# Splitting the last two weight tiles of each part into memory outside the ring, so that part ends split no weights

## The chip, the cores and the metric
One core of one Trainium2 chip runs the whole program. The metric is device time in microseconds; smaller is better. Three timed runs of the kernel before took 1474.11, 1475.65 and 1478.8 us (median 1475.65).

## What is computed
Two layers over a sequence of 256 tokens, width 1024, all in float32. Cut to what matters:

```python
for l in range(2):
    x = x + 0.5 * rms_norm(swiglu(rms_norm(x, ffn1_pre_g), ffn1_w_gu, ffn1_w_down), ffn1_post_g)
    x = x + rms_norm(hybrid_mixer(rms_norm(x, mix_pre_g), ...), mix_post_g)     # GLA, S5, forgetting attention
    x = x + rms_norm(memory_cross_attention(rms_norm(x, xa_pre_g), rms_norm(mem, xa_mem_g), ...), xa_post_g)
    x = x + 0.5 * rms_norm(swiglu(rms_norm(x, ffn2_pre_g), ffn2_w_gu, ffn2_w_down), ffn2_post_g)
```

## The kernel before
Each float32 matrix product is made of three products of two rounded halves: `mm3` multiplies high by high, high by low and low by high. So every weight has to be split into two halves on the chip, and that is a steady work beside the matmuls. `make_plan` lists all weights in the order of use as tiles of 128 x 1024. `fetch` brings a tile by a DMA on SyncE's queue into one of `WF` = 5 raw buffers (`wf`). `split_next` casts it on ScalarE to the high half `wh` (L221) and subtracts that from the raw tile to get the low half `wl` (L222), on VectorE (DVE) unless a caller names GpSimd (POOL). The two halves live in a ring of `WB` = 7 tile pairs. `take` hands out the next pair to the matmuls, `free` gives it back, and `ahead`, called between groups of matmuls, splits until the ring holds one pair less than it can (`lag=1`). Every engine does its instructions in the order in which the program lists them; nothing is rescheduled.

A layer has four parts, and each ends at a norm: the first FFN, the mixer up to `w_mix`, the cross attention (`xa`), the second FFN. The end of a part is `boundary`. The last `TAIL` = 5 weight tiles of the part are held together: `go_tail(0)` makes with them the last rows for tokens 0 to 127, `go_tail(1)` those for tokens 128 to 255. While the second runs, ACT, DVE and POOL make the norm of the first half of the tokens (`early`): squares of the finished banks (`junk`, L363), their sum (`rv`, L369), its power -1/2 on GpSimd (`rr`, L370), gain (`nw`, L382), residual sum (`x`, L394), the next norm (L401, L404), scaling (L409) and transposes on TensorE (L415), whose results are split into `xth` and `xtl`. The same chain for the second half (`late`) runs while TensorE makes the next part's first products for the first half (`head`, `go(0)`, L318: four weight tiles). Just before the end of `go(0)` (a hook at 46 of its 48 units of 256 columns) TensorE needs the scaled second half for the transposes `turn(1, 0)`; then `go(1)` follows.

With 5 tiles of the tail in a ring of 7, only two of the four head tiles can be split ahead of the tail. The third is split in `early` by

```python
            self.split_next(nc.gpsimd)
```

once the tail's first tile is given back, and the fourth by the same line ahead of `self.head(width)`. After the mixer there is no head: `fill` makes the first two key projections of the cross attention (`xa_key`, result `kT`) with four tiles `xa_k`, while `late` runs. There the third tile is split on GpSimd, the fourth on DVE, and while `self.pool_every = 4` every fourth tile that no caller names an engine for goes to GpSimd too. `merge_last`, ahead of the `w_mix` products, splits two tiles on GpSimd in each layer, and `first`, at the start of the program, two.

There are seven such boundaries: five with a head (after both FFNs of layer 0, the first of layer 1, and both cross attentions) and two with the fill (after both mixers). The second FFN of layer 1 ends in `store`.

## Time and profile before

| | |
|---|---|
| median of three runs | 1475.65 us |
| the profiled execution | 1474.54 us |
| its span, first to last instruction | 1472.8 us |
| mean granted TensorE clock | 0.989 |
| TensorE busy | 1428.6 us (97%) |
| VectorE busy | 937.3 us (64%) |
| ScalarE busy | 716.3 us (49%) |
| GpSimd busy | 121.2 us (8%) |
| DMA | 257.52 MB, mean 175 GB/s |

The profile is one execution. "Busy" is the sum of the instructions' times on an engine. A share tells little here: TensorE is busy at all but a few places, so what matters are the waits of TensorE and the granted clock behind them. 1474.54 us of the execution less 1472.8 us of span is 1.74 us around the program, in which no instruction of it lies.

### The profile page before, as it was taken

Reading aid. Unit: us, or ns where it says so; the run is one execution under the profiler, and the core shown is the slowest. Engines: PE = TensorE matmul, PEld = TensorE weight load, DVE = VectorE, ACT = ScalarE, POOL = GpSimd, SP = SyncE. Lnnn points to the kernel's source line nnn. Section 1 sums busy time; section 2 is a strip of 40 time slices with the busy share of each in tenths; the row PEclk is TensorE's granted clock in tenths of the full one; section 3 lists DMA queues with packets and bytes.
Section 4 is the critical chain, followed back from the end, with each engine's and each line's share of the span. In section 5 each row is a group of like instructions: output and inputs, shape, how many; then the busy total and the mean of one; then the engine's idle time right before and its main releaser. Section 6 shows DMA issues by size and latency. Waiting matters only on the chain.

```text
span 1472.8 us, 24677 instructions
## 1 busy us (share of the span) xinstructions
PE 1428.6 (97%) x9972; PEld 1318.5 (90%) x9972; DVE 937.3 (64%) x1388; ACT 716.3 (49%) x1129; POOL 121.2 (8%) x80
## 2 busy tenths in 40 slices
PE   8999998999999999999999999989999999999998
PEld 7999978889979989999999999788999798899997
DVE  6787566755486666555578675666556866665553
ACT  5444446355455545444454544454544644454442
POOL 1000020001141020000010000200012400200000
PEclk9999999999999999999999999999999999999999
DMA  7664636255546436555455555362565464275551
GB/s 280 214 199 148 211 108 213 92 156 181 192 173 231 156 113 232 193 178 188 156 181 207 171 200 187 117 191 90 158 229 175 154 216 158 91 248 190 180 192 45
DMA packets 76034, 257.52 MB, mean 175 GB/s; under 512 B 8688, under 2 KB 11792, under 8 KB 75920
## 3 DMA queue, kind: packets, MB, share of 16 engines
q1 hardware_dynamic: 75920, 255.95, 52.2%
q8 instruction: 78, 1.28, 0.3%
q14 instruction: 36, 0.29, 0.1%
HBM read 253.82 MB, written 2.10 MB: 174 GB/s over the span
## 4 chain that ended last, share of the span: by engine, by line
PE 85%; DVE 6%; ACT 4%; issue 2%; DMA 1%; POOL 1%; SPq 0%; DVEq 0%; POOLq 0%; ACTq 0%
PE mm L232 55%; PE pa L232 22%; PE mm L318 3%; DVE wl L222 2%; DVE x L394 1%; ACT wh L221 1%; PE mm L415 1%; DMA fq<-in_onehot 1%; ACT junk L363 1%; PE mm L1033 1%; DVE acc L1193 1%; PE mm L707 1%; DVE xtl L222 0%; PE mm L890 0%; PE pa L925 0%
## 5 line engine op out<-in xcount | busy, mean ns | idle before, releaser
L222 DVE TENSOR_TENSOR wl<-wf,wh 128x1024 fp32r<-128x1024 f32 x432 | 525.1, 1227 | 271.7 <-ACT wh L221 270.6
L232 PE MATMUL mm<-xth,wh 128*128 128x256 f32 (+1 forms) x2000 | 569.9, 285 | 0.0
L232 PE MATMUL mm<-xth,wl 128*128 128x256 f32 (+1 forms) x2000 | 567.2, 284 | 0.0
L232 PE MATMUL mm<-xtl,wh 128*128 128x256 f32 (+1 forms) x2000 | 566.2, 283 | 0.0
L221 ACT CAST wh<-wf 128x1024 fp32r<-128x1024 f32 (+1 forms) x458 | 463.0, 1030 | 161.1 <-PE mm L232 67.7
L232 PEld LDWEIGHTS mm<-xth,wh 128*128 128x128 f32 (+1 forms) x2000 | 378.7, 189 | 4.0 <-issue 2.1
L232 PEld LDWEIGHTS mm<-xtl,wh 128*128 128x128 f32 (+1 forms) x2000 | 376.9, 188 | 1.8
L232 PEld LDWEIGHTS mm<-xth,wl 128*128 128x128 f32 (+1 forms) x2000 | 377.5, 189 | 0.0
L232 PE MATMUL pa<-wh,hl 128*128 128x512 f32 x352 | 137.7, 391 | 0.0
L232 PE MATMUL pa<-wl,hh 128*128 128x512 f32 x352 | 137.6, 391 | 0.0
L232 PE MATMUL pa<-wh,hh 128*128 128x512 f32 x352 | 137.5, 391 | 0.0
L370 POOL TENSOR_TENSOR rr<-rv,mhalf 128x1 f32<-128x1 f32 x36 | 27.9, 775 | 885.5 <-DVE rv L369 876.7
L538 ACT ACTIVATE sil<-mm 128x256 f32<-128x256 f32 (+1 forms) x96 | 35.0, 365 | 127.3 <-PE mm L232 119.8
L540 DVE TENSOR_TENSOR h<-sil,mm 128x256 f32<-128x256 f32 (+1 forms) x96 | 38.0, 396 | 64.3 <-ACT sil L538 64.3
L232 PEld LDWEIGHTS pa<-wh,hl 128*128 128x128 f32 x352 | 66.1, 188 | 14.0
L232 PEld LDWEIGHTS pa<-wl,hh 128*128 128x128 f32 x352 | 66.1, 188 | 12.8
L232 PEld LDWEIGHTS pa<-wh,hh 128*128 128x128 f32 x352 | 66.2, 188 | 12.6
L221 ACT CAST hh<-h 128x256 fp32r<-128x256 f32 x80 | 32.5, 406 | 91.7 <-DVE h L540 91.7
L222 POOL TENSOR_TENSOR wl<-wf,wh 128x1024 fp32r<-128x1024 f32 x26 | 68.6, 2638 | 78.8 <-ACT wh L221 78.8
L222 DVE TENSOR_TENSOR hl<-h,hh 128x256 fp32r<-128x256 f32 x80 | 34.0, 425 | 37.8 <-ACT hh L221 37.8
L232 PE MATMUL pa<-wl,xth 128*128 128x512 f32 x128 | 50.9, 397 | 2.8 <-DVE wl L222 2.7
L232 PE MATMUL mm<-mt,wh 128*128 128x256 f32 x256 | 48.0, 290 | 5.1 <-DVE kT L222 5.1
(274 smaller groups left out, 1701.4 us busy)
## 6 DMA issues: line engine op xcount, KB each, us to landing
wf<-in_ffn_gu SPq DMA_DIRECT2D x176, 512.0 KB, 4.3
wf<-in_ffn_dn SPq DMA_DIRECT2D x88, 512.0 KB, 4.3
wf<-in_w_cols SPq DMA_DIRECT2D x72, 512.0 KB, 4.0
wf<-in_w_mix SPq DMA_DIRECT2D x16, 512.0 KB, 4.4
wf<-in_xa_k SPq DMA_DIRECT2D x16, 512.0 KB, 4.4
wf<-in_xa_q SPq DMA_DIRECT2D x16, 512.0 KB, 4.7
wf<-in_xa_v SPq DMA_DIRECT2D x16, 512.0 KB, 4.4
wf<-in_xa_o SPq DMA_DIRECT2D x16, 512.0 KB, 4.8
```

The source lines that it names most:

```text
L221: self.nc.scalar.copy(h, src)
L222: (eng or self.nc.vector).tensor_tensor(full(lo), src, h.bitcast(F32), op=ALU.subtract)
L232: self.nc.tensor.matmul(out, lhsT=lhs[i], rhs=rhs[j], start=start and n == 0, stop=stop and n == 2)
L318: self.nc.tensor.matmul(out, lhsT=xt[b][:, kk, tk], rhs=w[2 * g + i][a][:, k * width:(k + 1) * width], start=first, stop=last)
L363: self.nc.scalar.activation(jk, src, AF.Square, scale=math.sqrt(f / D), accum_out=s)
L370: self.nc.gpsimd.tensor_tensor(r, v, self.mhalf[:, 0:1], op=ALU.pow)
L394: self.nc.vector.scalar_tensor_tensor(xx, o, r, xx, op0=ALU.mult, op1=ALU.add)
L415: self.nc.tensor.transpose(ps[:, i * 128:(i + 1) * 128], hn[:, k * 128:(k + 1) * 128], self.ident)
L538: nc.scalar.activation(sil, gate, AF.Silu)
L540: nc.vector.tensor_tensor(h, sil, up, op=ALU.mult)
L707: T.matmul(ps[0:32, j * 128:(j + 1) * 128], lhsT=cz[:, i, 4 * q + j], rhs=wa[:, i, 4 * q + j].rearrange("p k h -> p (k h)"), start=i == 0, ...
L1033: T.matmul(o[:, 0:256], lhsT=fv[:, 0, c], rhs=p[:, 0:256], start=True, stop=False)
```

## The change
`make_plan` notes where each of the parts ends in the list of tiles. `house` gives the last two tiles of a part a home outside the ring: in the FFNs the tiles `e0`, `e1`, `e2` of the FFN's pool (in the first FFN these are also scratch of `s5_setup`, under new tags), after the mixer the places of `acc`, `m1` and `fv`, after the cross attention those of the keys (`foh`, `fol`, `fq`, `fk`). A tile with a home takes no place in the ring: `room` lets it be split whenever it is next, and only tiles in the ring are counted (`n_ring`). The `split_next` calls in `boundary` and `pool_every` are gone; the new `ahead(0)` at its start fills the ring.

```diff
+    def house(self, homes):
+        at = self.parts.pop(0)
+        for n, home in enumerate(homes):
+            self.homes[at - len(homes) + n] = home
+
+    def room(self, lag=0):
+        return self.n_split < len(self.plan) and (self.n_split in self.homes or self.n_ring < WB - lag)
...
-        assert i < self.n_free + WB
+        assert self.room()
...
-        h = self.wp.tile([128, HALF], F32R, tag="wh", name="wh")
-        lo = self.wp.tile([128, HALF], F32R, tag="wl", name="wl")
+        if i in self.homes:
+            h, lo = self.homes[i]()
+        else:
+            self.n_ring += 1
+            h = self.wp.tile([128, HALF], F32R, tag="wh", name="wh")
+            lo = self.wp.tile([128, HALF], F32R, tag="wl", name="wl")
...
     def ahead(self, lag=1):
-        while self.n_split < min(len(self.plan), self.n_free + WB - lag):
+        while self.room(lag):
             self.split_next()
...
-        while self.n_split < min(len(self.plan), self.n_free + WB):
-            self.split_next()
+        self.ahead(0)
         go_tail(0)
...
             st["p1"][0](0)
-            self.split_next(nc.gpsimd)
             self.scale(h0, r0)
...
         if fill is not None:
-            self.split_next()
             late()
...
-        self.split_next(nc.gpsimd)
         ps, go = self.head(width)
...
+        self.house((two_halves, lambda: [pool.tile([128, HALF], F32R, tag=n, name="we") for n in ("e1", "e2")]))
...
+        self.house([lambda ns=ns: [com.tile([128, HALF], F32R, tag=n, name="we") for n in ns]
+                    for ns in (("foh", "fol"), ("fq", "fk"))])
...
-                    self.pool_every = 4
+                    self.house((mix_home, lambda: [p.tile([128, HALF], F32R, tag=n, name="we")
+                                                   for p, n in ((self.per, "m1"), (com, "fv"))]))
```

GpSimd's order, from the first boundary to the first fill of layer 0. Before (`rr` is the power -1/2, `wl` a split, `acc` a sum of the mixer):

```order
L370 TENSOR_TENSOR rr<-rv,mhalf 128x1 x2
L222 TENSOR_TENSOR wl<-wf,wh 128x1024
L370 TENSOR_TENSOR rr<-rv,mhalf 128x1
L222 TENSOR_TENSOR wl<-wf,wh 128x1024
L370 TENSOR_TENSOR rr<-rv,mhalf 128x1
L860 TENSOR_TENSOR orr<-ov,mhalf 128x8
```

and with the change (lines have moved by 18 to 20):

```order
L388 TENSOR_TENSOR rr<-rv,mhalf 128x1 x4
L880 TENSOR_TENSOR orr<-ov,mhalf 128x8
```

Both splits have left the boundary. In the whole program 20 of GpSimd's 26 splits are gone; the two of `first` and the four of `merge_last` stay.

VectorE's order at the end of the first mixer, from the last split of the mixer's output (`xtl`) to the residual sum of the first half. Before (`mt` is the transposed memory, `nw<-pa,gain` the first step of the boundary's chain):

```order
L1190 SCALAR_TENSOR_TENSOR xtl<-acc,xth 128x512
L222 TENSOR_TENSOR wl<-wf,wh 128x1024 x2
L222 TENSOR_TENSOR mt<-mm,mt 128x4x128 x2
L222 TENSOR_TENSOR wl<-wf,wh 128x1024
L222 TENSOR_TENSOR mt<-mm,mt 128x4x128 x2
L222 TENSOR_TENSOR wl<-wf,wh 128x1024
L382 TENSOR_TENSOR nw<-pa,gain 128x512
L369 TENSOR_SCALAR rv<-ss 128x1
L382 TENSOR_TENSOR nw<-pa,gain 128x512
L394 SCALAR_TENSOR_TENSOR x<-nw,rr,x 128x512 x2
```

and with the change (`we` is a tile in a home):

```order
L1210 SCALAR_TENSOR_TENSOR xtl<-acc,xth 128x512
L240 TENSOR_TENSOR wl<-wf,wh 128x1024 x2
L240 TENSOR_TENSOR we<-wf,we 128x1024 x2
L240 TENSOR_TENSOR wl<-wf,wh 128x1024
L240 TENSOR_TENSOR mt<-mm,mt 128x4x128 x2
L240 TENSOR_TENSOR wl<-wf,wh 128x1024
L240 TENSOR_TENSOR mt<-mm,mt 128x4x128 x2
L240 TENSOR_TENSOR wl<-wf,wh 128x1024 x2
L400 TENSOR_TENSOR nw<-pa,gain 128x512
L387 TENSOR_SCALAR rv<-ss 128x1
L400 TENSOR_TENSOR nw<-pa,gain 128x512
L412 SCALAR_TENSOR_TENSOR x<-nw,rr,x 128x512 x2
```

Eight splits stand here on VectorE instead of four, five of them ahead of the first `mt`.

VectorE's order after the scaling of the second half in the same boundary, up to the second `kT`. Before:

```order
L222 TENSOR_TENSOR wl<-wf,wh 128x1024
L394 SCALAR_TENSOR_TENSOR x<-nw,rr,x 128x512 x2
L401 TENSOR_TENSOR nw<-x,gain 128x512
L369 TENSOR_SCALAR rv<-ss 128x1
L404 TENSOR_TENSOR nw<-x,gain 128x512
L409 TENSOR_SCALAR nw<-nw,rr 128x512 x2
L222 TENSOR_TENSOR wl<-wf,wh 128x1024 x3
L222 TENSOR_TENSOR kT<-mm,kT 128x512
L222 TENSOR_TENSOR wl<-wf,wh 128x1024
L222 TENSOR_TENSOR kT<-mm,kT 128x512
```

and with the change:

```order
L412 SCALAR_TENSOR_TENSOR x<-nw,rr,x 128x512 x2
L419 TENSOR_TENSOR nw<-x,gain 128x512
L387 TENSOR_SCALAR rv<-ss 128x1
L422 TENSOR_TENSOR nw<-x,gain 128x512
L427 TENSOR_SCALAR nw<-nw,rr 128x512 x2
L240 TENSOR_TENSOR wl<-wf,wh 128x1024 x4
L240 TENSOR_TENSOR kT<-mm,kT 128x512
L240 TENSOR_TENSOR wl<-wf,wh 128x1024 x2
L240 TENSOR_TENSOR kT<-mm,kT 128x512
```

The split ahead of the second `x` has gone; ahead of the two `kT` six splits stand on VectorE instead of four (before, two of the six were GpSimd's).

## Rows read from the trace of the kernel before

**Rows 1.** The page: the span, and busy time of the engines with share of the span and instructions.
```profile
span 1472.8 us, 24677 instructions
PE 1428.6 (97%) x9972; PEld 1318.5 (90%) x9972; DVE 937.3 (64%) x1388; ACT 716.3 (49%) x1129; POOL 121.2 (8%) x80
```

**Rows 2.** Waits of TensorE by what ended them: us in total, times, longest us.
```profile
PE mm L415 <- DVE nw L409: 11.8, 5, 2.5
```

**Rows 3.** TensorE in order of time: the first instruction after a wait, at the five heads (L415), in the tail of the first mixer (425.62), and at the third key projection of both fills (451.59 and 1179.69). Columns: start us, us, engine, line, operation, shapes, count; in brackets the idle time before it and what ended it.
```profile
217.57 0.66 PE L415 MATMUL mm<-cst,nw 128*128 128x128 f32 x4 [2.50 <-DVE nw L409]
552.72 1.09 PE L415 MATMUL mm<-cst,nw 128*128 128x128 f32 x4 [2.21 <-DVE nw L409]
745.98 0.63 PE L415 MATMUL mm<-cst,nw 128*128 128x128 f32 x4 [2.33 <-DVE nw L409]
944.84 0.84 PE L415 MATMUL mm<-cst,nw 128*128 128x128 f32 x4 [2.50 <-DVE nw L409]
1282.30 0.63 PE L415 MATMUL mm<-cst,nw 128*128 128x128 f32 x4 [2.21 <-DVE nw L409]
425.62 0.50 PE L232 MATMUL pa<-wl,xth 128*128 128x512 f32 x1 [1.37 <-DVE wl L222]
451.59 0.50 PE L232 MATMUL mm<-mt,wh 128*128 128x256 f32 x2 [1.52 <-DVE kT L222]
1179.69 0.50 PE L232 MATMUL mm<-mt,wh 128*128 128x256 f32 x2 [3.63 <-DVE kT L222]
```

**Rows 4.** VectorE and GpSimd in order of time at the first boundary: the residual sums of the first and the second half of the tokens, and a split on GpSimd. Columns as in rows 3.
```profile
203.71 1.41 DVE L394 SCALAR_TENSOR_TENSOR x<-nw,rr,x 128x512 f32<-128x512 f32 x2
211.38 3.55 DVE L394 SCALAR_TENSOR_TENSOR x<-nw,rr,x 128x512 f32<-128x512 f32 x2
...
211.51 2.86 POOL L222 TENSOR_TENSOR wl<-wf,wh 128x1024 fp32r<-128x1024 f32 x1 [0.54 <-ACT wh L221]
```

**Rows 5.** The residual sums of the whole run, by line: count, then shortest, median and longest of one in ns, first and last start in us.
```profile
L394 DVE SCALAR_TENSOR_TENSOR x<-nw,rr,x x28: 741/746/2893, 203.7 to 1276.7; 128x512 f32<-128x512 f32 x28
```

**Rows 6.** Stretches of TensorE: start and end in us, length, busy us of PE, PEld, DVE, ACT and POOL with their instructions, then the granted clock, DMA share and GB/s. In order: the first boundary (512 wide) from the transposes of the first half to the wait, and from the wait to the end of `go(1)`; the same two at the second boundary (256 wide); behind the wait of the first fill; behind that of the second.
```profile
207.89:215.07 7.18, 7.18 (x35) 5.51 (x34) 6.64 (x9) 3.47 (x8) 5.95 (x3) 1.00 0.21 73
217.57:225.90 8.33, 8.32 (x33) 6.80 (x34) 6.62 (x8) 6.09 (x8) 0.00 (x0) 0.80 0.36 112
542.80:550.51 7.71, 7.69 (x58) 6.88 (x56) 6.74 (x9) 3.76 (x8) 5.79 (x3) 1.00 0.21 72
552.72:561.17 8.45, 8.45 (x58) 8.45 (x59) 6.12 (x7) 5.91 (x7) 0.00 (x0) 0.80 0.23 72
451.59:453.60 2.01, 2.01 (x16) 2.01 (x17) 1.07 (x1) 1.11 (x2) 0.00 (x0) 1.00 0.94 253
1179.69:1184.20 4.51, 4.51 (x25) 4.51 (x26) 4.00 (x5) 0.65 (x1) 0.00 (x0) 0.62 0.88 301
```

**Rows 7.** The chain that ended last: a tail of the first FFN, 57 matmuls of 512 columns. Start us, us, what.
```profile
195.09 12.96 PE pa L232 x57
```

**Rows 8.** The splits by engine and shape: count, busy us, mean ns of one, idle time before them and what ended it.
```profile
L222 DVE TENSOR_TENSOR wl<-wf,wh 128x1024 fp32r<-128x1024 f32 x414 | 513.3, 1250 | 253.6 <-ACT wh L221 252.5
L222 POOL TENSOR_TENSOR wl<-wf,wh 128x1024 fp32r<-128x1024 f32 x26 | 68.6, 2638 | 78.8 <-ACT wh L221 78.8
```

**Rows 9.** ScalarE in order of time at the end of the first mixer: the casts of the fourth to sixth `w_mix` tile (counted from 0), and those of two `xa_k` tiles, ahead of the first square of the boundary. Columns as in rows 3.
```profile
417.58 2.94 ACT L221 CAST wh<-wf 128x1024 fp32r<-128x1024 f32 x3
423.27 2.01 ACT L221 CAST wh<-wf 128x1024 fp32r<-128x1024 f32 x2
426.39 0.60 ACT L363 ACTIVATE junk<-pa 128x512 bf16<-128x512 f32 x1 [1.10 <-PE pa L232]
```

**Rows 10.** VectorE at the same boundary: a split, the first gain, the two residual sums with their scalings, and the splits ahead of `kT`.
```profile
418.65 1.22 DVE L222 TENSOR_TENSOR wl<-wf,wh 128x1024 fp32r<-128x1024 f32 x1 [0.25 <-ACT wh L221]
428.83 0.68 DVE L382 TENSOR_TENSOR nw<-pa,gain 128x512 f32<-128x512 f32 x1
431.53 1.42 DVE L394 SCALAR_TENSOR_TENSOR x<-nw,rr,x 128x512 f32<-128x512 f32 x2
435.14 0.88 DVE L409 TENSOR_SCALAR nw<-nw,rr 128x512 f32<-128x512 f32 x2 [0.44 <-POOL rr L370]
440.82 1.41 DVE L394 SCALAR_TENSOR_TENSOR x<-nw,rr,x 128x512 f32<-128x512 f32 x2
444.42 0.88 DVE L409 TENSOR_SCALAR nw<-nw,rr 128x512 f32<-128x512 f32 x2 [0.44 <-POOL rr L370]
445.22 5.71 DVE L222 TENSOR_TENSOR wl<-wf,wh 128x1024 fp32r<-128x1024 f32 x3
```

**Rows 11.** TensorE there: the transposes of the first half (the hook of the tail), and the start of the first key projection.
```profile
435.95 0.60 PE L415 MATMUL mm<-cst,nw 128*128 128x128 f32 x4
437.44 0.48 PE L232 MATMUL mm<-mt,wh 128*128 128x256 f32 x2
```

**Rows 12.** DMA issues of the page: count, KB each, median us from issue to landing; and SyncE's longest wait for splits of GpSimd (us in total, times, longest us).
```profile
wf<-in_xa_k SPq DMA_DIRECT2D x16, 512.0 KB, 4.4
...
SPq L147 <- POOL wl L222: 133.3, 24, 12.7
```

**Rows 13.** The end of the values' projection in the first cross attention: VectorE's low halves of the second half of `v`, and TensorE's first product that reads them.
```profile
518.45 1.38 DVE L222 TENSOR_TENSOR v<-mm,v 128x512 fp32r<-128x512 f32 x2 [0.31 <-ACT v L221]
...
521.12 1.59 PE L232 MATMUL mm<-pt,v 128*128 128x256 f32 x12
```

More of the change, by code (lines that the diff above doesn't have):

```diff
@@ L80, in make_plan @@
         a = self.a
-        self.plan = []
+        self.plan, self.parts = [], []
         def add(ap, n=2048):
@@ L98, in ffn @@
                 add(dn[l, k], D)
+            self.parts.append(len(self.plan))
         for l in range(depth):
@@ L133, in make_plan @@
                 add(a["w_mix"][l, q])
+            self.parts.append(len(self.plan))
             for n in ("xa_k", "xa_q", "xa_v", "xa_o"):
@@ L136, in make_plan @@
                     add(a[n][l, q])
+            self.parts.append(len(self.plan))
             ffn(l, 2)
-        self.n_dma = self.n_split = self.n_take = self.n_free = 0
-        self.raw, self.ready = {}, {}
+        self.n_dma = self.n_split = self.n_take = self.n_free = self.n_ring = 0
+        self.raw, self.ready, self.homes = {}, {}, {}
         self.pool_every = 0
+    def house(self, homes):
[4 more added lines that the diff above has]
+        return self.n_split < len(self.plan) and (self.n_split in self.homes or self.n_ring < WB - lag)
     def fetch(self, upto):
@@ L177, in free @@
     def free(self, n=1):
-        self.n_free += n
+        for _ in range(n):
+            self.n_ring -= self.n_free not in self.homes
+            self.n_free += 1
     def start(self, gen, first=False):
@@ L528, in ffn, with two_halves @@
         hs = [None] * NFT
+        def two_halves():
+            t = pool.tile([128, 2, HALF], F32R, tag="e0", name="we")
+            return t[:, 0], t[:, 1]
+        self.house((two_halves, lambda: [pool.tile([128, HALF], F32R, tag=n, name="we") for n in ("e1", "e2")]))
         def split_h(j, src):
@@ L671, in times @@
                 3).to_broadcast([128, 8, m, 32])
-        wa = t8(2, 8, 4, 32)
-        w1, w2 = t8(8, 4, 32), t8(8, 4, 32)
+        wa = pool.tile([128, 2, 8, 4, 32], F32, tag="e0", name="wa")
+        w1, w2 = [pool.tile([128, 8, 4, 32], F32, tag=n, name=n) for n in ("e1", "e2")]
         a3, b3 = w1[:, :, 0:3], w2[:, :, 0:3]
@@ L1342, in run, with mix_home @@
                     pairs = [(xt[0][:, k], xt[1][:, k]) for k in range(KT)]
-                    self.pool_every = 4
+                    def mix_home():
+                        t = lp.tile([128, 2, HALF], F32R, tag="acc", name="we")
+                        return t[:, 0], t[:, 1]
+                    self.house((mix_home, lambda: [p.tile([128, HALF], F32R, tag=n, name="we")
+                                                   for p, n in ((self.per, "m1"), (com, "fv"))]))
                     for k in range(0, KT - TAIL, 2):
@@ L1349, in run @@
                     xt, _ = self.boundary(banks, tail, False, fill=lambda q: self.xa_key(q, mt, kt))
-                    self.pool_every = 0
                     self.start(self.gains(a["xa_post_g"][l], a["ffn2_pre_g"][l]))
```

## Prediction, made before the changed kernel was run
> **What bounds the kernel now.** I read the page first. TensorE is busy in 97% of the span and VectorE in 64% [rows 1], so the change can only be worth what TensorE loses at particular places, and VectorE has room for more work if it comes where nobody waits. The waits of TensorE by what ended them come next: the largest group is the transposes of the second half, which wait for VectorE's scaling, 11.8 us in five waits [rows 2]. In order of time these are the five heads, 2.21 to 2.50 us each; at the fills TensorE waits 1.37 us in the tail, and 1.52 and 3.63 us ahead of the third key projection [rows 3]. Then I went back along VectorE at the first boundary: the pair of residual sums of the first half takes 1.41 us, that of the second 3.55 us, and in the second case a split on GpSimd runs from 211.51 to 214.37 [rows 4]. Over the run the sum has a median of 746 ns and a longest of 2893 ns [rows 5]; two normal ones in a row overlap a little (1.41 us). Last the granted clock: the stretches behind the heads' waits have a mean of 0.80, those ahead of them 1.00; behind the 1.52 us wait it stayed at 1.00, behind the 3.63 us one it was 0.62 [rows 6]. The two levels are 2.4 and 1.2 GHz, so a wait of some 2.2 us or more is paid for twice here, and one of 1.5 us only once.
>
> **Heads: the stall.** The change takes both of GpSimd's splits out of the boundary. The second residual sum then has nothing beside it on GpSimd and should take what the first takes: 3.55 - 1.41 = 2.14 us less on the chain sum, squares, power, scaling, transposes. All five waits are longer than that (shortest 2.21) [rows 3], so 5 x 2.14 = **10.7 us**. 0.07 to 0.36 us of wait are left at each. The two casts that also leave ScalarE stood in gaps and count nothing.
>
> **Heads: the clock.** With waits this short the clock should stay up. The price is bounded from two sides. Above: the slow stretches lost their missing share of the clock, 0.20 x 8.45 = 1.69 and 0.20 x 8.33 = 1.67 us [rows 6], 3 x 1.69 + 2 x 1.67 = 8.4 us for three heads of 256 columns and two of 512. Below: the stretch ahead of the wait does nearly the same work at full clock, and also waits a little for the split of the activations, which slow matmuls hide. 57 matmuls of 512 columns take 12.96 us, 0.23 each [rows 7]. At 256 columns the first stretch has 46 matmuls and 3 of 512, the second 50: one of 512 less for each two of 256, so 7.71 - 0.24 = 7.47 against 8.45, 0.98 us. At 512 columns it has 26 against 25: 7.18 - 0.23 = 6.95 against 8.33, 1.38 us. 3 x 0.98 + 2 x 1.38 = **5.7 us**. I take this one, since it is measured on the same work.
>
> **Where the splits go.** 20 splits move from GpSimd (2.64 us each) to VectorE (1.22 us without stalls) [rows 8, 10], 24.4 us of VectorE's time. In the FFNs the two homes make one burst of three splits, in the second last projection: two casts more on ScalarE, 2.44 us more on VectorE, whose next product is a little late, but its result is needed only in the tail. Zero. Per boundary the DMAs and casts are the same in number, only earlier; SyncE's queue keeps its order and loses the 133.3 us for which it waited on GpSimd's splits [rows 12]. I cost that at nothing, since the ring is full when it happens.
>
> **Cross attention.** There the burst of three stands ahead of the split of `v`. VectorE ended that at 518.45 + 1.38 = 519.83; with 2 x 1.22 more, less its idle gap of 0.31, at some 522.0, while TensorE began to read it at 521.12, its second low half about half a microsecond later [rows 13]. Between 0 and 0.9 us each, taken as 0.2: **-0.4 us** for both layers.
>
> **Fills.** This is the place with two answers. Casts go at 2.94 / 3 = 0.98 us or a little less from 417.58 on ScalarE, splits from 418.65 on VectorE [rows 9, 10]. Now eight splits and four `mt` stand ahead of the first gain, where four splits did, two of them slowed by GpSimd. VectorE: five splits to 424.7, two `mt` to 426.0, a split, two `mt`, two splits: 430.6, against 428.83 before [rows 10]. The last two raw tiles can only be fetched when the burst frees buffers (421 and 422), and land 4.4 us later [rows 12], more when they queue: about 427.6, so the last cast ends at 428.6 and delays the first square from 426.39 [rows 9]. The residual sum then starts at 432.1, not 431.53 (before, it waited for the square anyway), the scaling at 435.7, not 435.14, its first half is ready at 436.2.
> TensorE no longer waits 1.37 us in the tail (the low half of the last tile is done at 423.5), so it comes to the hook at 435.95 - 1.37 = 434.6, waits 1.6 us and goes on at 436.2, 0.25 us later than before [rows 3, 11]. From there VectorE gains: no split ahead of the second residual sum, so that starts 0.9 us earlier and the scaling at 443.5. Four splits of 1.2 us follow where three took 5.71 us beside GpSimd [rows 10]: `kT` is done at 449.8. TensorE reaches the third projection at 437.44 + 0.25 plus the 12.63 us between these points (451.59 - 1.52 - 437.44), 450.3, and does not wait. Gain 451.59 - 450.3 = 1.3 us in layer 0, and with the longer wait (3.63) 1.3 + 2.1 = 3.4 in layer 1, plus its slow clock, 0.38 x 4.51 = 1.7 us [rows 6], since that work is dense. **6.4 us.**
>
> **Sum.** 10.7 + 5.7 - 0.4 + 6.4 = 22.4 us. The profiled execution took 1474.54 us, so 1452.1. It lies 1.1 us below the median of the three runs (1475.65), and what is predicted is a median: **1453 us**.
>
> **Rivals.** *The fills' new wait lowers the clock.* My 1.6 us at the hook lies between 1.52 (clock stayed) and 2.21 (clock fell) [rows 3, 6]. If it falls in both, 2 x 1.7 us come back: 1456.4. The Trainium skill speaks for this one (TensorE: Matmul & The Clock Gate, What's actually happening): the gate judges activity in windows that run freely, so how an idle time falls into them decides; by that even a wait as short as those that held here may cost. The rows show none under 2.21 us that did.
> *The fills gain nothing* (raw tiles land later than 4.4 us, the squares wait, what is saved at `kT` is lost at the hook): 1453 + 6.4 = 1459.4. For it speaks that ScalarE takes casts in order, so a late tile holds back the squares.
> *GpSimd's split is not what slows the residual sum*: then the five waits and slow clocks stay, 1453 + 10.7 + 5.7 = 1469.4. Against it: one of each pair is normal, and the first pair, with no split beside it, is normal in both [rows 4].
> *Slower.* The fourth head tile's cast now stands ahead of the squares on ScalarE at all seven boundaries. If its raw tile landed 10 us after its buffer is free instead of 4.4, each chain could start 5.6 us later: 7 x 5.6 = 39.2 us against 22.4 gained, 1475.65 + 16.8 = 1492.5. It decides from (22.4 + 4.4) / 7 = 3.8 us of lateness at each boundary on. Against it: the landings of such tiles have a median of 4.4 us [rows 12], and the burst frees the buffers earlier than single splits would.
> That the splits would stay where they are is excluded by the order of instructions.
>
> **Chances.** Forecast 0.66; clock at the fills 0.14; fills without gain 0.12; residual sum unchanged 0.04; slower 0.04. No change means within 0.3% (4.4 us, about what a measurement of this kernel can tell), 1471.2 to 1480.1. The first three cases lie clear below (0.92). The fourth lies at the edge, so half of it is faster and half no change; of the fifth a quarter is no change. Faster 0.94, same 0.03, slower 0.03. The range starts at 1447: 2.7 us for the upper bound of the clock, 1.6 if the hook does not wait, and 1.7 for the scatter of the median. It ends at 1460, above the second rival. That leaves out less than 2 in 10.
>
> **What would show it.** Right: all 28 residual sums near 746 ns; the waits of L415 under 0.5 us and a clock of 1.00 behind them; no wait for `kT`; GpSimd with 6 splits; VectorE's busy time up by about 24.4 us less the stalls; a wait of some 1.6 us at the hook of both fills (new group, transposes of the first half), with the clock at 1.00 behind it. Wrong: a residual sum still at 2.9 us, a clock of 0.80 behind short waits, or a first square of the boundary that waits for a DMA through the cast ahead of it.

## The result, and the profile after

The changed kernel takes **1457.44 us** (median of four runs, 1456.21 to 1458.61) against 1474.88 of the kernel before (four runs): a ratio of 0.9882, 95% interval 0.9864 to 0.9901, or 17.4 us less. The forecast was 1453.0 in a range of 1447 to 1460. The profiled execution after took 1458.61 us.

The page of the kernel after, answering to [rows 1] (span; busy us, share of the span and instructions by engine):
```profile
span 1456.8 us, 24663 instructions
...
PE 1425.2 (98%) x9972; PEld 1314.7 (90%) x9972; DVE 936.4 (64%) x1408; ACT 715.2 (49%) x1129; POOL 68.8 (5%) x60
```
GpSimd lost 20 instructions and VectorE gained them, yet VectorE is no busier (937.3 us before). The splits, by line, engine and shape (count, busy us, mean ns), show why; they answer to [rows 8]:
```profile
L240 DVE TENSOR_TENSOR wl<-wf,wh 128x1024 fp32r<-128x1024 f32 x418 | 508.3, 1228 | 246.4 <-ACT wh L239 245.4
L240 DVE TENSOR_TENSOR we<-wf,we 128x1024 fp32r<-128x1024 f32 x16 | 18.8, 1217 | 0.0
...
L240 POOL TENSOR_TENSOR wl<-wf,wh 128x1024 fp32r<-128x1024 f32 x6 | 14.9, 2482 | 47.3 <-ACT wh L239 47.3
```
`we` is a split into a home, sixteen in all; the other four that GpSimd lost go into the ring. VectorE now makes 434 splits for 508.3 + 18.8 = 527.1 us; before, 414 took 513.3. Twenty more cost 13.8 us, not 24.4, because the ones beside GpSimd no longer stall. The residual sums, by line (count; shortest, median, longest in ns), save most of the rest, 5 x 2.1 us; this is the row that answers to [rows 5]:
```profile
L412 DVE SCALAR_TENSOR_TENSOR x<-nw,rr,x x28: 739/744/753, 203.9 to 1263.8; 128x512 f32<-128x512 f32 x28
```
The five long ones of 2.9 us are gone. TensorE's waits by what ended them (us in total, times, longest), of which [rows 2] showed one group before:
```profile
PE pa L821 <- DVE dg L815: 9.9, 2, 5.0
PE mm L433 <- DVE nw L427: 6.0, 7, 2.5
...
PE pa L967 <- DMA yv<-yd: 1.7, 1, 1.7
...
PE pa L967 <- issue: 0.7, 1, 0.7
```
The seven waits of L433 in order of time (start, length, engine, line, operation, shapes, count; idle before it and what ended it) are the five heads of [rows 3] and, second and sixth, the two fills, where no such wait stood before. There it is the hook in the tail, the transposes of the first half (the expectations below call it the fills' second hook):
```profile
215.80 0.66 PE L433 MATMUL mm<-cst,nw 128*128 128x128 f32 x4 [0.45 <-DVE nw L427]
...
434.94 0.63 PE L433 MATMUL mm<-cst,nw 128*128 128x128 f32 x4 [1.96 <-DVE nw L427]
...
549.51 0.63 PE L433 MATMUL mm<-cst,nw 128*128 128x128 f32 x4 [0.17 <-DVE nw L427]
...
739.53 0.63 PE L433 MATMUL mm<-cst,nw 128*128 128x128 f32 x4 [0.29 <-DVE nw L427]
...
935.37 0.66 PE L433 MATMUL mm<-cst,nw 128*128 128x128 f32 x4 [0.44 <-DVE nw L427]
...
1152.89 1.09 PE L433 MATMUL mm<-cst,nw 128*128 128x128 f32 x4 [2.55 <-DVE nw L427]
...
1267.40 0.63 PE L433 MATMUL mm<-cst,nw 128*128 128x128 f32 x4 [0.17 <-DVE nw L427]
```
Stretches behind the first head, behind the fifth, and behind the two fills' hooks, as in [rows 6] (length; busy us of PE, PEld, DVE, ACT, POOL; granted clock, DMA share, GB/s):
```profile
215.46:223.50 8.04, 7.69 (x37) 5.92 (x38) 6.89 (x9) 6.08 (x8) 0.00 (x0) 1.00 0.36 106
...
1267.20:1276.00 8.80, 8.63 (x70) 8.20 (x70) 7.51 (x9) 6.57 (x8) 0.00 (x0) 1.00 0.35 116
...
434.94:440.00 5.06, 5.06 (x28) 4.77 (x29) 4.12 (x9) 2.28 (x5) 0.55 (x1) 0.66 0.00 0
1152.89:1158.00 5.11, 5.11 (x28) 4.71 (x29) 3.36 (x7) 1.76 (x4) 0.55 (x1) 0.69 0.00 0
```
The clock stays at 1.00 (2.4 GHz) behind the heads, where it was 0.80, and now falls behind the fills' hooks. The waits in the tail and for `kT` ([rows 3], last three) are gone. VectorE at the first fill, answering to the first gain, sum and scaling of [rows 10], shows where the hook's time went:
```profile
429.16 0.68 DVE L400 TENSOR_TENSOR nw<-pa,gain 128x512 f32<-128x512 f32 x1
...
430.69 1.41 DVE L412 SCALAR_TENSOR_TENSOR x<-nw,rr,x 128x512 f32<-128x512 f32 x2
...
434.31 0.88 DVE L427 TENSOR_SCALAR nw<-nw,rr 128x512 f32<-128x512 f32 x2 [0.44 <-POOL rr L388]
```
TensorE came to the hook at 434.94 - 1.96 = 432.98, 3.0 us earlier than before, but the scaling started only 0.83 us earlier. From the split at 417.46 to the first gain VectorE paused for less than 0.2 us; the eight splits and four `mt` fill that time. The casts of the last two tiles on ScalarE also waited for their DMAs, 1.01 and 0.31 us, and the first square followed right behind them, without a wait for TensorE:
```profile
426.93 1.05 ACT L239 CAST wh<-wf 128x1024 fp32r<-128x1024 f32 x1 [0.31 <-DMA wf<-in_xa_k]
427.88 0.59 ACT L381 ACTIVATE junk<-pa 128x512 bf16<-128x512 f32 x1
```
VectorE lost 0.13 us to that here. At the second fill these casts waited 1.65 and 0.33 us, and VectorE 0.63 us for them, about what the hook there waits longer (2.55 against 1.96):
```profile
1144.59 1.23 DVE L240 TENSOR_TENSOR wl<-wf,wh 128x1024 fp32r<-128x1024 f32 x1 [0.48 <-ACT wh L239]
1145.97 1.23 DVE L240 TENSOR_TENSOR wl<-wf,wh 128x1024 fp32r<-128x1024 f32 x1 [0.15 <-ACT wh L239]
```

**The ledger.** TensorE makes the same 9972 products in the same order in all these kernels, so the start of the n-th product before, less its start in another kernel, is what that kernel has gained up to there. The differences over the segments of the program, in us, one profiled execution each (negative: lost):
```
                 five heads  fill 0  fill 1  recurrence 0  recurrence 1   rest   total
before, again        2.29     0.03    0.00      -1.36         -0.78      -0.38   -0.22
after               15.50     0.05    3.18      -1.64         -0.81      -0.35   15.93
after, again        15.44    -0.11    5.33      -1.09         -2.02      -0.10   17.46
heads_only          15.11    -0.01    0.00      -1.02         -3.86      -0.06   10.15
fill_only            4.33     1.80    3.42      -0.87          0.03       0.09    8.80
fill_only, again     4.44     1.35    3.57      -0.57         -0.97       0.09    7.91
vector_splits        1.75    -1.43   -1.44      -1.09         -2.79       0.49   -4.52
read_beside          9.12    -0.11    4.64      -0.55         -1.37      -0.19   11.54
copy_beside         13.52     1.70    3.70      -1.18         -2.04       0.01   15.72
write_beside        15.43    -0.04    3.30       0.18         -2.00      -0.51   16.36
k3_late             15.50     2.32    6.01      -1.39         -2.47      -0.82   19.15
k2k3_late           15.43     2.88    6.47      -1.22         -1.05      -0.33   22.19
```
"Recurrence" is the mixer's stretch from behind the head through the recurrence (L821) and the read-back of `yv` (L967). Against the prediction's terms: heads 16.4 forecast, 15.5 here; fills 6.4 forecast, 3.2 here; the recurrences, for which there was no term, -2.5. The first row is the measure of chance: the kernel before, once more, loses 2.1 us at the recurrences with nothing changed. The later kernels were timed in other sessions, each with runs of the kernel before beside them, so they are compared by their ratios.

### The profile page after: what moved, and what is told of

Read it like the earlier page. It is cut to its first block, busy times and chain, and to the rows that moved or that the text cites. A ratio compares the mean times of both kernels' runs of the same rounds, so it can differ in the third digit from the quotient of the medians.

```text
span 1456.8 us, 24663 instructions
## 1 busy us (share of the span) xinstructions
PE 1425.2 (98%) x9972; PEld 1314.7 (90%) x9972; DVE 936.4 (64%) x1408; ACT 715.2 (49%) x1129; POOL 68.8 (5%) x60
## 4 chain that ended last, share of the span: by engine, by line
PE 86%; DVE 5%; ACT 4%; issue 2%; DMA 2%; POOL 1%; SPq 0%; DVEq 0%; POOLq 0%; ACTq 0%
PE mm L250 57%; PE pa L250 21%; PE mm L336 3%; ACT wh L239 1%; DVE wl L240 1%; PE mm L433 1%; DMA wf<-in_xa_k 1%; ACT junk L381 1%; DVE acc L1213 1%; POOL rr L388 1%; PE mm L1053 1%; PE mm L727 1%; PE pa L945 0%; PE mm L910 0%; DVE xtl L1210 0%
## 5 line engine op out<-in xcount | busy, mean ns | idle before, releaser
L240 DVE TENSOR_TENSOR wl<-wf,wh 128x1024 fp32r<-128x1024 f32 (+1 forms) x436 | 520.2, 1206 | 264.6 <-ACT wh L239 263.6
L239 ACT CAST wh<-wf 128x1024 fp32r<-128x1024 f32 (+1 forms) x442 | 446.0, 1029 | 154.3 <-PE mm L250 63.4
L250 PE MATMUL pa<-wh,hl 128*128 128x512 f32 x320 | 125.3, 392 | 0.0
L250 PE MATMUL pa<-wl,hh 128*128 128x512 f32 x320 | 125.2, 391 | 0.0
L250 PE MATMUL pa<-wh,hh 128*128 128x512 f32 x320 | 124.8, 390 | 0.0
L250 PEld LDWEIGHTS pa<-wh,hl 128*128 128x128 f32 x320 | 60.0, 188 | 12.7
L250 PEld LDWEIGHTS pa<-wl,hh 128*128 128x128 f32 x320 | 60.1, 188 | 11.9
L250 PEld LDWEIGHTS pa<-wh,hh 128*128 128x128 f32 x320 | 60.2, 188 | 11.6
L239 ACT CAST xth<-mm 128x512 fp32r<-128x512 f32 x39 | 22.6, 587 | 54.7 <-PE mm L433 23.6
L240 DVE TENSOR_TENSOR xtl<-mm,xth 128x512 fp32r<-128x512 f32 x40 | 27.2, 688 | 27.8 <-ACT xth L239 27.8
```

The lines of the kernel that those rows point to most:

```text
L239: self.nc.scalar.copy(h, src)
L240: (eng or self.nc.vector).tensor_tensor(full(lo), src, h.bitcast(F32), op=ALU.subtract)
L250: self.nc.tensor.matmul(out, lhsT=lhs[i], rhs=rhs[j], start=start and n == 0, stop=stop and n == 2)
```

## The experiments

My theory after the result: the heads' gain comes from taking a GpSimd operation out from beside VectorE's residual sum; the fills gave what was forecast, but lost about half of it at the hook to VectorE's two more splits and to the clock. Rivals: that VectorE's or ScalarE's share of the splits mattered and not GpSimd; that the homes alone count; that the clock follows simply from the length of a wait.

**Each part alone.** heads_only: the mixer's end as before.
```diff
-                    self.house((mix_home, lambda: [...]))
+                    self.house(())
+                    self.pool_every = 4
```
with `self.split_next(nc.gpsimd)` in `early()` and `self.split_next()` ahead of `late()` again where `fill` is given. fill_only is the reverse: `self.house(())` in both FFNs and the cross attention, GpSimd's two splits again where `fill` is not given.

> The homes of the FFNs and of the cross-attention stay, the mixer's end is as in the kernel before (GpSimd splits, every fourth tile on GpSimd, the fourth xa_k tile split behind the boundary). Theory (the heads' gain is the GpSimd split taken from beside the residual sums; the fills give about 0 in layer 0 and 3 us in layer 1): the residual sums of the heads at 740 to 760 ns, the heads' waits under 0.5 us, no granted clock under 0.9 behind a head, the fills' waits as before (1.4 to 1.5 us on the last splits, 1.5 us at the second hook), the sum in the fills at 2.9 us; 1458 to 1461 us, ratio to before 0.989 to 0.991. Rival 1 (the fills' own gain of 6.4 us stands as the prediction had it, and something else in the changed kernel ate it): 1463 to 1465 us. Rival 2 (the fills cost more than they gave, through their lost clock): 1453 to 1456 us.

Measured: 1463.85 us, ratio 0.9917 (0.9904 to 0.9931), a gain of 10.7 us. The range was missed, and the time lies in that of rival 1. The heads behave as expected (15.1 in the ledger, waits of 0.4 us and less), and the fills' waits are those of before, but 1.0 and 3.9 us go in the two recurrences, the larger at the read-back (TensorE, then the stretch's clock):
```profile
1030.10 3.55 PE L970 MATMUL pa<-yv,glw 128*128 128x256 f32 x8 [1.91 <-issue]
```
```profile
1030.00:1035.00 5.00, 4.90 (x21) 4.28 (x22) 0.69 (x1) 1.31 (x3) 0.00 (x0) 0.67 0.35 85
```


> Homes only at the mixer's end, GpSimd splits nothing there; all other part ends split on GpSimd as in the kernel before. Theory: heads as before (waits 2.2 to 2.5 us, residual sum 2.9 us, clock 0.80 behind them); fills with no wait on the last splits and a second-hook wait of 1.9 to 2.6 us with a clock drop behind each; gain 0 to 4 us: 1471 to 1475 us, ratio 0.997 to 1.000. Rival 1 (the fills alone give the 6.4 us of the prediction): 1468 us, no clock drop behind the hook. Rival 2 (they cost): over 1476 us.

Measured: 1466.86 us, 0.994 (0.9928 to 0.9953), a gain of 7.7 us, nearest to rival 1 in time and to neither in mechanism. The fills give 5.2 us in the ledger; their hooks wait 1.75 and 2.25 us, and only the second is followed by a low clock, where the theory had both. Another 4.3 come at heads that were not touched. TensorE's waits there are as before, in order of time:
```profile
217.53 0.66 PE L433 MATMUL mm<-cst,nw 128*128 128x128 f32 x4 [2.50 <-DVE nw L427]
...
550.71 0.63 PE L433 MATMUL mm<-cst,nw 128*128 128x128 f32 x4 [2.22 <-DVE nw L427]
...
742.86 0.63 PE L433 MATMUL mm<-cst,nw 128*128 128x128 f32 x4 [2.30 <-DVE nw L427]
...
940.48 0.66 PE L433 MATMUL mm<-cst,nw 128*128 128x128 f32 x4 [2.49 <-DVE nw L427]
...
1273.45 0.63 PE L433 MATMUL mm<-cst,nw 128*128 128x128 f32 x4 [2.22 <-DVE nw L427]
```
and the stretches behind them (columns as above) keep the clock in four of five:
```profile
217.00:225.40 8.40, 7.86 (x39) 6.11 (x40) 7.25 (x9) 6.32 (x8) 0.00 (x0) 1.00 0.41 121
549.50:558.00 8.50, 7.29 (x58) 6.91 (x58) 6.77 (x9) 5.93 (x7) 0.54 (x1) 1.00 0.31 103
741.60:750.00 8.40, 7.14 (x57) 6.74 (x58) 6.67 (x9) 5.92 (x7) 0.59 (x1) 1.00 0.29 100
939.30:947.70 8.40, 7.21 (x33) 5.52 (x34) 6.80 (x10) 5.60 (x8) 0.60 (x1) 1.00 0.35 117
1273.00:1281.50 8.50, 8.04 (x55) 8.08 (x56) 6.63 (x8) 5.93 (x7) 0.00 (x0) 0.80 0.26 80
```
So the rule that I read from [rows 6], that a wait of 2.2 us lowers the clock, was too strong. Two second profiles settle whether that is chance.

> The kernel before once more, for a second profile. If the low clock behind the five heads follows from the length of the wait in front of it: 3.4 us of low clock behind each of the five again. If a wait of 2.2 to 2.5 us lowers the clock only at some executions: fewer than five, other places, and the ledger of this execution is shorter by about 1 us for each that is missing.

> fill_only once more, for a second profile: its heads' waits of 2.2 to 2.5 us stand in a kernel whose first profile had the low clock behind one of five. If chance: another number and other places, waits unchanged within 0.2 us. If something in fill_only keeps the clock up behind its heads: one or none again, at the same places.

Measured: 1474.78 and 1466.64 us. In the kernel before, stretches behind the five heads now read:
```profile
217.05:225.40 8.35, 7.41 (x30) 6.25 (x31) 5.75 (x8) 5.48 (x7) 0.36 (x1) 0.80 0.28 88
552.50:561.00 8.50, 6.70 (x43) 6.49 (x44) 6.77 (x10) 5.73 (x7) 0.86 (x1) 0.80 0.31 96
743.00:751.00 8.00, 5.66 (x45) 5.05 (x44) 6.01 (x9) 3.34 (x6) 2.20 (x2) 1.00 0.22 81
942.00:950.00 8.00, 5.51 (x27) 3.81 (x26) 6.16 (x11) 4.68 (x8) 0.93 (x2) 1.00 0.24 72
1281.50:1290.00 8.50, 7.54 (x51) 7.57 (x52) 5.88 (x8) 5.76 (x7) 0.30 (x1) 0.80 0.20 64
```
Three of five where it had been five of five, with waits of 2.21 to 2.51 us in both; fill_only has one of five again, but behind the second head, not the fifth:
```profile
551.00:559.50 8.50, 8.50 (x60) 8.50 (x60) 6.62 (x8) 5.92 (x7) 0.00 (x0) 0.80 0.28 91
```
It is chance in where, and the two executions of the kernel before are as long as each other: the 2.3 us that the heads did not lose went at the recurrences (-1.4 in layer 0, where the low stretch behind the 5 us wait of L801 lasted twice as long, and -0.8 in layer 1). Why fill_only had one low head twice and the kernel before three and five is not settled by four profiles.

**Is it GpSimd's place?** vector_splits is the kernel before, with the two splits on VectorE:
```diff
-            self.split_next(nc.gpsimd)
+            self.split_next()
...
-        self.split_next(nc.gpsimd)
+        self.split_next()
```


> The kernel before, with the boundary's two GpSimd splits made by VectorE at the same places of the program; ring and number of splits unchanged, no homes. Theory (GpSimd beside the sum costs 2.15 us per head; the split itself is an ordinary 1.2 us of VectorE in the same chain): residual sums 740 to 760 ns, heads' waits 2.2 to 2.5 less 2.15 plus 1.2 = 1.3 to 1.6 us, and no clock drop behind them, as none stood behind the 1.52 us wait of the kernel before: gain 5 x 0.95 + 5.7 = 10.4, 1463 to 1466 us, ratio 0.992 to 0.994. If a wait of 1.5 us does lower the clock here: gain 4.7, about 1470 us. Rival (the homes are what counts, GpSimd's place does not): waits stay over 2 us, 1474 us or more.

Measured: 1478.54 us, 1.0023 (1.0011 to 1.0034), slower by 4 us; forecast missed by 12 us and more, and the rival not met either. The sums, and TensorE's two hooks at the first boundary:
```profile
L394 DVE SCALAR_TENSOR_TENSOR x<-nw,rr,x x28: 743/747/754, 203.3 to 1284.3; 128x512 f32<-128x512 f32 x28
```
```profile
208.99 0.66 PE L415 MATMUL mm<-cst,nw 128*128 128x128 f32 x4 [1.36 <-DVE nw L409]
...
217.88 0.66 PE L415 MATMUL mm<-cst,nw 128*128 128x128 f32 x4 [1.69 <-DVE nw L409]
```
The sums are normal, and the second hooks of the heads wait 1.41 to 1.69 us instead of 2.21 to 2.50, near the 1.3 to 1.6 of the forecast, with no low clock behind them. What I had left out is the other split: on VectorE it stands ahead of the first half's scaling, so the first hook, which did not wait before, waits 1.19 to 1.47 us at all seven boundaries (-1.4 us at each fill). By the ledger 2.9 us go at the fills and 3.9 at the recurrences, and the heads gain only 1.75. So GpSimd's split was free at the first hook and dear at the second, and the homes are worth having because they take both off this chain.

**What of GpSimd's work blocks the sum?** Three kernels put one GpSimd operation of 128 x 1024 back into the changed kernel, ahead of `head`, on a gain tile that nobody reads any more. read_beside has a subtraction, copy_beside `tensor_copy(gpost, gpost)` and write_beside `memset(gpost, 0.0)` in that line:
```diff
+        nc.gpsimd.tensor_tensor(gpost, gpost, gpost, op=ALU.subtract)
         ps, go = self.head(width)
```


> The changed kernel, with one GpSimd tensor_tensor (128 x 1024, in place on the gain tile that is dead by then) put back where the GpSimd split stood ahead of each head; no weights move. Theory (a GpSimd operation that reads and writes while VectorE makes the residual sum stretches that sum to GpSimd's own length): the second residual sum at 2.5 to 2.9 us, heads' waits 1.8 to 2.5 us, clock 0.80 behind them; gives back 10.7 + 5.7 = about 16: 1470 to 1475 us. Between, if the clock holds: 1467 us. Rival (what counted was VectorE's or ScalarE's share of the splits, or their data): sums 740 to 760 ns, 1457 to 1459 us.

> The changed kernel with one GpSimd memset (128 x 1024, of the gain tile that is dead by then) where read_beside had its tensor_tensor: GpSimd writes as much and reads nothing. Theory A (it is any GpSimd access beside the sum that stretches it): second residual sum longer than 750 ns by about the memset's length less 0.7 us, as under the 1.90 us tensor_tensor, which made it about 1.9 us; time 1459 to 1463 us. Theory B (it takes a GpSimd operation that reads two tensors): all 28 sums at 740 to 760 ns, heads' waits under 0.5 us, time as the changed kernel, 1456.5 to 1458.5 us.

> As write_beside, but GpSimd copies the 128 x 1024 tile onto itself: one tensor read, one written. Theory (what blocks VectorE's two-tensor sum is a GpSimd operation that reads, and the sum ends about 0.55 us behind it): the sum that starts inside the copy ends 0.5 to 0.6 us after the copy's end; if the copy takes 0.95 us as the memset did, a sum of about 1.0 us, waits up by 0.3 us per head, 1456 to 1459 us. Rival (only a GpSimd operation with two inputs blocks): all sums at 740 to 760 ns.

The GpSimd operation and the pair of sums at the first boundary, in order of time, in read_beside:
```profile
211.04 1.90 POOL L490 TENSOR_TENSOR gain<-gain 128x1024 f32<-128x1024 f32 x1
...
211.47 2.67 DVE L412 SCALAR_TENSOR_TENSOR x<-nw,rr,x 128x512 f32<-128x512 f32 x2
```
in copy_beside:
```profile
210.83 1.04 POOL L490 COPY gain<-gain 128x1024 f32<-128x1024 f32 x1
...
211.28 1.80 DVE L412 SCALAR_TENSOR_TENSOR x<-nw,rr,x 128x512 f32<-128x512 f32 x2
```
and in write_beside:
```profile
211.32 0.95 POOL L490 MEMSET gain<- 128x1024 f32 x1
...
211.77 1.41 DVE L412 SCALAR_TENSOR_TENSOR x<-nw,rr,x 128x512 f32<-128x512 f32 x2
```
read_beside took 1462.14 us (ratio to before 0.9911, 0.9898 to 0.9925), copy_beside 1458.89 (0.9898, 0.987 to 0.9925), write_beside 1455.52 (0.9876, 0.9857 to 0.9894). The longest sum, by its line, is 2008 ns beside the tensor_tensor, 1137 beside the copy and 754 beside the memset, and 2893 beside the split of before [rows 5]. A sum that starts inside a reading GpSimd operation ends 0.54 to 0.56 us after it: 211.47 + 2.01 against 211.04 + 1.90 in read_beside, 211.28 + 1.14 against 210.83 + 1.04 in copy_beside, 212.04 + 2.89 against 211.51 + 2.86 before. It is blocked for the rest of that operation, whatever its length; one input is enough. The memset, nearly as long as the copy and as early, blocks nothing. In [rows 4] the first sum of the late pair started 0.13 us ahead of GpSimd's split and was normal, the second started inside it. The Trainium skill (SBUF — State Buffer, Who interferes with whom) says that a VectorE instruction with two SBUF inputs contends with a GpSimd instruction that reads SBUF and not with one that only writes, and that the one that starts second is blocked entirely; by that, all four cases come out as measured. write_beside's 1455.52 us lies 1 us below the range of theory B; its sums decide for B against A, and copy_beside's then show that one tensor read is enough, where B asked for two.

For read_beside I had expected a sum of 2.5 to 2.9 us and 1470 us or more. The mechanism held and the size did not: the tensor_tensor takes 1.90 us, not a split's 2.86, so each head loses 1.3 us (15.5 - 9.1 in five), and at its waits of 1.43 to 1.73 us the clock stayed up (1.00 from 216.9 to 225.4). copy_beside loses 0.4 us per head, write_beside none (15.43).

**The fills.** k3_late splits the fourth `xa_k` tile behind `late()` again, k2k3_late the third one too, inside `early()`; both on VectorE, homes unchanged:
```diff
-        self.ahead(0)
+        self.ahead(0 if fill is None else 2)
...
             st["p1"][1](0)
+            if fill is not None:
+                self.split_next()
...
         if fill is not None:
             late()
+            self.split_next()
```
This is k2k3_late; k3_late has 1 for the 2 and nothing new in `early()`. The added split in `early()` stands behind the multiplication of the second half, and thus behind the scaling of the first. (In vector_splits it stood ahead of it.)

> The changed kernel, but ahead of the mixer's tail only one of the two tiles is split early; the fourth xa_k tile is split behind late() again, as before, on VectorE. Theory (the fills gave the 6.4 us of the prediction and lost 3.1 of it to VectorE's splits in front of the second hook, one such split being about 1.2 us): second-hook waits of the two fills 0.7 to 1.4 us instead of 1.96 and 2.55, no clock drop behind them, no new wait for the last split in front of the fill: 1453 to 1455.5 us. Rival (the late split stands in front of kT again and brings the old 1.5 to 3.6 us wait back): 1456 to 1459 us.

> As k3_late, and the third xa_k tile too is split later, inside the first hook behind VectorE's first multiplication (where GpSimd split one before). Theory: second-hook waits under 0.5 us, no clock drop: 1451.5 to 1454.5 us. Rival 1 (the split inside the hook delays the first half of the turn, as the 1.4 us waits at the first hooks of vector_splits): 1455 to 1459 us.

Measured: 1453.89 us (0.9865, 0.9846 to 0.9885) and **1452.19 us** (0.9856, 0.9838 to 0.9874), both in the expected range. The waits at the hooks come near what was expected: 0.62 and 0.60 us in k3_late (0.7 to 1.4 expected), 0.66 and 0.76 in k2k3_late (under 0.5 expected). The hooks of k2k3_late, on TensorE in order of time, and the stretch behind the second:
```profile
433.17 0.63 PE L433 MATMUL mm<-cst,nw 128*128 128x128 f32 x4 [0.66 <-DVE nw L427]
...
1148.09 0.63 PE L433 MATMUL mm<-cst,nw 128*128 128x128 f32 x4 [0.76 <-DVE nw L427]
...
1148.09:1154.00 5.91, 5.91 (x47) 5.73 (x48) 5.82 (x10) 2.88 (x7) 0.55 (x1) 1.00 0.27 89
```
No low clock stands behind them (1.00 from 431 to 440, too), no wait for `kT` came back, and the fills give 2.9 + 6.5 = 9.4 us of the ledger instead of 3.2 (5.2 in the changed kernel's second profile). Of the 6.1 us between 3.2 and 9.4, the shorter waits at the hooks are 3.1 and the low clock behind them the rest. A split that is moved takes its cast and its tile's DMA along, so by itself this edit does not tell VectorE's work from the late tiles. VectorE's rows above do: at the first fill it was busy without them, at the second they add 0.6 us. In k3_late a wait for `kT` did come back, small:
```profile
PE mm L250 <- DVE kT L240: 0.7, 2, 0.4
```
The third split's move took that away and left the hooks as they were; it is worth 0.5 us at each fill. So the fills' part of the change was worth more than was forecast, and two splits in the wrong place took 4 to 6 us of it. Against the kernel before k2k3_late gains 21.5 us, the changed kernel 17.4; the difference of 4 us is not wholly clear of the noise, as their intervals (0.9838 to 0.9874, 0.9864 to 0.9901) overlap.

**The changed kernel's second profile.**

> The changed kernel once more, for a second profile. If the clock's drops are fixed by the work in front of them: low clock behind both fills (3.4 us each) and 6.8 us behind the first recurrence of layer 0 again, the read-back in layer 0 late by 1.7 us again. If a wait of 2 to 2.6 us lowers the clock only at some executions (as the heads of fill_only say, where waits of 2.2 to 2.5 us did so once in five): other places or lengths of the low clock, at waits that are the same within 0.2 us.

Measured: 1457.1 us. The heads give 15.44 (15.50 in the first profile). The hook of the first fill was again followed by a low clock (wait 2.11 us, 1.96 in the first profile). That of the second was not; it waited 1.91 us instead of 2.55, as VectorE did not wait for a late tile there, and this fill gives 5.33 instead of 3.18. The read-back was late in the second layer by 1.7 us instead of the first. The heads' terms repeat to a tenth; the clock's and those of DMAs that land late do not, so neither answer that was expected is wholly met.

## Why the prediction was right, and where it was off

- **Heads, 16.4 forecast, 15.5 measured.** The stall and the clock can be told apart now. At the four heads of fill_only that kept the clock, the ledger shows 1.03 to 1.22 us of gain at an unchanged wait, and at two heads of before_again 1.22 and 1.04: one low stretch costs 1.1 us, five 5.4 (forecast 5.7, from the lower bound; the upper one, 8.4, is excluded). Its share by width was not as forecast: 1.03 and 1.05 us at the two heads of 512 columns (1.38 forecast), 1.14 and 1.22 at those of 256 (0.98). The stall is the remainder, 15.5 - 5.4 = 10.1 (forecast 10.7); the five waits themselves fell by 2.04 to 2.06 us each, 10.2 in all. What is not shown is that the clock's 5.4 is a steady part of the gain: the low stretches at the heads are five, three, one and one in four profiles with the same waits. That the term came out near its size is in part luck: measured against the second profile of the kernel before, with three low heads, the heads give 15.5 - 2.3 = 13.2 us, not 15.5.
- **Where the splits go, 0, and cross attention, -0.4.** Held: all that lies outside the heads, fills and recurrences sums to -0.35 in the first profile and -0.10 in the second. By parts it is otherwise: in both profiles the ends of the two first FFNs lose 0.25 us each, where nothing was forecast, and the cross attentions 0.1 in all.
- **Fills, 6.4 forecast, 3.2 measured (5.2 in the second profile).** The step that failed is that the hook's wait of 1.6 us would leave the clock at 1.00. The chain on VectorE was right: the kernel after was 1.18 us ahead when the first fill began, so on the prediction's base its scaling starts at 434.31 + 1.18 = 435.5, against 435.7, and TensorE goes on at 434.94 + 1.18 = 436.1, against 436.2. TensorE came at 432.98 + 1.18 = 434.2 instead of 434.6, since by the ledger the tail gave 1.9 us and not 1.37, so the wait was 1.96. In layer 1 it was 2.55, for the late tiles. The clock fell behind both waits, which by the ledger cost 1.5 and 1.3 us, 2.8 of the 3.2 that are missing; the late tiles of layer 1 are 0.6, and the rest gained a little more than forecast. The clock's fall is rival 1, priced at 1456.4, with 1457.4 measured; that the two are so near is in part luck, as the measured time also holds what the recurrences lost. Over all kernels whose fills have such a hook wait, 1.75 to 2.58 us, the clock fell in nine of fourteen cases, so its chance of 0.14 looks too low; none of these waits was as short as the forecast 1.6. The Trainium skill's point (TensorE: Matmul & The Clock Gate, What's actually happening), that the gate's windows run freely, stood beside this rival; it fits that the same 2.2 to 2.5 us wait at the heads lowered the clock in ten of twenty cases, though no run shows the windows themselves.
- **What had no term: the recurrences, -2.5 us.** Behind the unchanged 5 us wait of L821 the low clock lasted twice as long in layer 0 (about 1 us), and the read-back of `yv` landed late. From issue to first use it took 7.1 and 6.7 us before, and 8.6 and 7.6 after, though nothing in the change touches it. The kernel before, once more, also loses 2.1 us at the same two places, so it is not shown that the 2.5 comes from the change. The lateness, in all of a kernel's read-backs, is 0 to 1.3 us in the six profiles whose heads still stall, and 0.6 to 2.4 us in the seven where they are free. The two ranges overlap. Whether arriving earlier, or the weights' transfers that stand elsewhere in time, makes it late stays open; it was not tried.
- **The other rivals.** That the fills gain nothing would have given 1459.4, in reach by the time alone, but k2k3_late shows the fills' 9.4. That GpSimd isn't the cause is excluded by the sums of read_beside, copy_beside and write_beside. The slower case, a raw tile late ahead of the squares, did not occur at the heads, where the first square waits for TensorE. At the fills the sign named for it, a first square behind a cast that waits for a DMA, did appear, as the prediction's own working of the fills had it; it cost VectorE 0.13 us at the first fill, whose first gain started at 429.16, which is 430.3 on the prediction's base, where 430.6 was forecast, and 0.63 at the second.
- **The sum.** 22.4 forecast against 15.9 by the profiled executions: 0.9 at the heads, 3.2 at the fills, 2.5 at the recurrences (rounded). The second profile has 17.5 and the medians differ by 17.4.

## What to carry to other kernels

Before moving work between VectorE and GpSimd, look at what reads two tensors on VectorE while GpSimd reads: here a residual sum that started inside such a GpSimd instruction waited for its end, so that instruction cost by its remaining length and its place, not by GpSimd's load. When splits are moved off one chain, follow them to the next one: what was free at five places cost 4 to 6 of 9.4 us at the sixth and seventh, and behind the scaling instead of ahead of it, on the same engine, nearly nothing. Follow their DMAs too: a tile that lands late holds up what stands behind its cast. Price a clock that falls behind a wait as a chance, not as a rule, until several profiles agree, and take a second profile of the kernel before, to know which differences come without a change.

## What the runs showed of the hardware that was not expected

- The same wait of TensorE, 2.2 to 2.5 us, was followed by the 1.2 GHz clock in 5, 3, 1 and 1 of five places in four profiles of two kernels; none of the waits of 1.7 us in read_beside was, yet 1.96 and 2.11 us at the first fill of the changed kernel were, in its two profiles, and 1.91 us at the second fill was not, nor was the longest such wait, 2.58 us at the second fill of read_beside. In two executions of the kernel before the low stretches stood in different places and the time was the same within 0.3 us.
- A GpSimd copy with one input blocks VectorE's sum as a two-input operation does; it is only shorter (1.04 against 1.90 us for 128 x 1024).
- The read-back of `yv` took 6.3 to 8.75 us from its issue to TensorE's first use over 13 profiles of nearly the same program; TensorE waited for it, by 0.2 to 1.9 us, in eleven of them.
